# A two-block transformer kernel: input sums of the feed-forwards in another order, squares added on VectorE, x stored from ScalarE's queue and loaded ahead, the first pair's weight sums made sooner

## The chip, the cores and the metric

The kernel runs on one core of one Trainium2 chip. The metric is the device time of one execution in microseconds (us). The engines are TensorE (PE for matmuls, PEld for weight loads), VectorE (DVE), ScalarE (ACT), GpSimd (POOL) and SyncE (SP, which only issues DMAs). TensorE's granted clock has two levels here, 2.4 and 1.2 GHz; the profile gives it as a fraction of the higher one.

## The reference, cut to what matters

Two transformer blocks run on a sequence of 512 tokens with 1024 channels. The change touches the places where a residual sum ends and the next normalised feed-forward (or attention) begins:

```python
x = x + jnp.einsum('bsd,de->bse', merged, w_out[l])       # block 1, residual
h2 = rmsnorm(x, norm_mlp_g[l])
up = jnp.square(jax.nn.relu(jnp.einsum('bsd,df->bsf', h2, w_up[l])))
x = x + jnp.einsum('bsf,fd->bsd', up, w_down[l])
...
x = x + merged @ w_mix_out[l]                              # block 2
x = x + cross_attention(rms_norm(x, xattn_norm_g[l]), ...) # its last step is "@ w_o"
x = x + swiglu(rms_norm(x, ffn_norm_g[l]), w_ffn_gate[l], w_ffn_up[l], w_ffn_down[l])
```

`rmsnorm` divides by the root of the mean square over the channels and multiplies by a gain per channel.

## The kernel before, in words

Activations lie transposed: a tile has 128 channels on the partitions and 512 tokens along the row, so x is 8 tiles (m = 0 to 7). Every fp32 operand is split into a high and a low part (`split_to`, lines 269 to 276: the high part by a cast on ACT, the low part by a subtraction on DVE), and a product is three matmuls (`mm3`). A projection to one tile (`proj_T`) takes a weight slab of 128 x 1024: it is loaded into a `raw` buffer from SP's queue, cast to `wh` on ACT (L270) and subtracted to `wl` on DVE (L271), and 24 matmuls of 512 columns follow. There are 3 `raw`, 4 `wh` and 4 `wl` buffers; the DMAs of weights stay in program order on SP.

**Two transitions** are the subject. In the first, `residual_stage` multiplies by `w_out` (tiles m = 0 and 1 together in `proj_T_lead`, then m = 2 to 7), reloads x from DRAM tile by tile on POOL's queue (L681), adds it to the product in PSUM (L683, DVE), stores the new x to a DRAM buffer on POOL's queue (`put`, L319) and calls `norm_sums`. In the second, `residual_keep` does the same for `w_xo`, with x still on chip, so without the load (the addition is L1517). A third place, `residual_stage` with `w_mix`, loads x too but calls `norm_tile` and stores nothing.

`norm_sums` prepares the input of a feed-forward whose matrix products are made by a fast scheme with seven half-size products in place of eight (indices 1 to 7). An even tile gives `ae` = x times gain (ACT); an odd tile gives `ao`, and from the two come the sums `f1` and `f2` (four DVE operations on half tiles, L346 to L349) and the splits of `s1` (half of `ae`), `f1`, `f2` and `ao`. `square` takes x squared on ACT (L472) and adds it to a running sum on POOL (L474); `rstd_tok` makes the last addition (L484, POOL), sums over the channels by 8 small matmuls against ones, and makes the root in some ten small DVE operations and the diagonal tiles `dgh`, `dgl`; `rstd_row` turns these into a row by two matmuls.

`weight_sums` loads two weight slabs and makes the sums and splits for the same scheme (L367 to L378: four casts on ACT, eight operations on DVE, with one `wh`, two `wl`, two `sum` and four `big` buffers). `halves` calls it and then makes the seven products into the PSUM tiles `u`, `v` and `p2`. For the first two jobs of a feed-forward (`halves_lead`) the parts that need no more than tiles 0 to 6 of x come first: all of product 1, and three quarters of products 5 and 2. These are 30 matmuls of 256 columns for each job; the rest waits for the last odd tile.

Instructions are written in program order, and a scheduler fixes each engine's order beforehand, by program order and its own estimate of when inputs are ready. On the chip an engine runs its list in that order, so an instruction that waits holds up all behind it on its engine; the same holds for DMAs in an engine's queue. Buffers of one kind are handed out as earlier users are done.

Of the kernel before, what the change touches and what calls it, by code (L numbers as in the profile page):

```python
# [15 lines left out]
S = 512  # L16
# [78 lines left out]
class Net:  # L95
    def __init__(self, tc, I, out, opts=None):
        self.tc, self.nc, self.I, self.out = tc, tc.nc, I, out
        self.o = dict(

            raw=3, wh=4, wl=4, sum=2, big=8, slots=56,  # L100

            attn=54, attn2=77, tail=30, early=8, adelay=23.0, lru=387, fox=40, fd=15.0, swa=44, cross=45,

            lL=6.63, lu=3.2, lo=8.0, lg=1.25, f0=1.6, f1=2.8, f2=1.4, s0=2.4, s1=6.9, s2=3.4, x1=5.75, x2=2.5,
        )
        self.o.update(opts or {})
        self.n = 0
        self.clock = Clock()
        self.sq = None


    def name(self, s):
# [203 lines left out]
    def put(self, m, x):  # L316
        if m == 0:
            self.xs = self.dp.tile([8, P, S], F32, tag="xs", bufs=1, name=self.name("xs"))
        self.nc.gpsimd.dma_start(out=self.xs[m], in_=x)  # L319

    def get(self, m):
        x = self.T("x")
# [3 lines left out]
    def norm_sums(self, x, g, kt, sq, st):  # L326


        nc = self.nc
        H = S // 2  # L330
        if kt % 2 == 0:
            a = self.T("ae")
            nc.scalar.activation(a, x, AF.Copy, scale=self.col(g, kt))
            self.square(x, sq)
            st["even"] = a
            return
        e, o = st.pop("even"), self.T("ao")
        nc.scalar.activation(o, x, AF.Copy, scale=self.col(g, kt))
        self.square(x, sq)
        kp = kt // 2  # L340
        if kp % 2 == 0:
            st["one"] = (self.R("s1h"), self.R("s1l"))
        c = (kp % 2) * H
        s1 = tuple(t[:, c : c + H] for t in st["one"])
        f1, f2 = self.T("f1"), self.T("f2")
        nc.vector.tensor_sub(f1[:, :H], e[:, H:], o[:, H:])  # L346
        nc.vector.tensor_sub(f1[:, H:], f1[:, :H], e[:, :H])
        nc.vector.tensor_sub(f2[:, :H], e[:, :H], e[:, H:])
        nc.vector.tensor_add(f2[:, H:], o[:, :H], f1[:, H:])  # L349
        self.split_to(s1[0], s1[1], e[:, :H])  # L350
        p1, p2, po = self.split(f1, s="f1"), self.split(f2, s="f2"), self.split(o, s="ao")
        cut = lambda p, i: tuple(t[:, i * H : i * H + H] for t in p)
        st.setdefault("S", []).append(
            {1: s1, 2: cut(po, 0), 4: cut(po, 1), 5: cut(p1, 0), 6: cut(p1, 1), 7: cut(p2, 0), 3: cut(p2, 1)}
        )
# [36 lines left out]
    def halves(self, wname, j, st, out, lead=False):  # L392

        nc = self.nc
        H = S // 2
        w = self.weight_sums(wname, j)
        u, v, p2 = self.PS("u"), self.PS("v"), self.PS("p2")
        if lead:
            late = range(KT // 2 - 1, KT // 2)
            early = range(KT // 2 - 1)  # L400
        a, b = self.T("ca"), self.T("cb")
        self.product(u, st, w, 1, True)
        nc.scalar.copy(a[:, :H], u[:, :H])
# [12 lines left out]
        self.product(u, st, w, 6, False)  # L416
        nc.scalar.copy(b[:, :H], u[:, :H])
        yield
        self.product(u, st, w, 7, False)
        nc.scalar.copy(b[:, H:], u[:, :H])  # L420
        nc.vector.tensor_sub(b[:, H:], v[:, :H], b[:, H:])
        yield
        self.product(u, st, w, 4, False)
        nc.scalar.copy(a[:, H:], u[:, :H])
        self.product(v, st, w, 3, False)
        nc.vector.tensor_sub(b[:, :H], v[:, :H], b[:, :H])
        if lead:
            yield
        out(a, b)

    def halves_lead(self, jobs):

        a, b = jobs
        for _ in range(3):
            next(a)
            next(b)
        r = self.rstd_tok(self.sq)
        for g in (a, b, a):
            next(g)
        self.r, self.row = self.rstd_row(r)  # L440
        self.sq = None
        self.rounds((a, b))
# [21 lines left out]
        for f in fillers:  # L464
            f()

    def square(self, x, sq, n=S, at=0):

        nc = self.nc
        q = self.T("sq")  # L470
        sl = slice(at, at + n)
        nc.scalar.activation(q[:, sl], x[:, sl], AF.Square)  # L472
        if len(sq) == 2:
            nc.gpsimd.tensor_add(sq[0][:, sl], sq[0][:, sl], sq[1][:, sl])  # L474
            sq.pop()
        sq.append(q)

    def rstd_tok(self, sq, n=S, at=0, quick=False):

        nc = self.nc  # L480
        nt = n // P
        if len(sq) == 2 and not quick:
            sl = slice(at, at + n)
            nc.gpsimd.tensor_add(sq[0][:, sl], sq[0][:, sl], sq[1][:, sl])  # L484
            sq.pop()
# [88 lines left out]
    def block1(self):  # L574
# [74 lines left out]
        for m in range(8):  # L649
# [6 lines left out]
        self.residual_stage("w_out", mg, "norm_mlp_g", self.I["xT"], True)  # L656

    def until(self, gen, cond):

# [10 lines left out]
        for g in gens:  # L670
            yield from g

    def residual_stage(self, wname, act, g, reload, halves=False):

        nc = self.nc
        sq = []
        new, nact, st = [], [], {}
        pss = self.proj_T_lead([(wname, 0), (wname, 1)], act)
        for m in range(8):
            x = self.T("x")  # L680
            nc.gpsimd.dma_start(out=x, in_=reload[m])  # L681
            ps = pss[m] if m < 2 else run(self.proj_T(wname, m, act))
            nc.vector.tensor_add(x, ps, x)  # L683
            new.append(x)
            if halves:
                self.put(m, x)
                self.norm_sums(x, g, m, sq, st)
            else:
                nact.append(self.norm_tile(x, g, m, sq))
        self.x, self.act, self.sq = [None] * 8 if halves else new, st if halves else nact, sq  # L690

    def consts1(self):
        nc = self.nc
# [816 lines left out]
    def residual_keep(self, wname, act, g):  # L1510
# [263 lines left out]
```

## Time and profile before

| | |
|---|---|
| median of 3 runs | 1924.06 us (1923.16 to 1924.74) |
| profiled execution | 1925.78 us, span of its trace 1924.0 us |
| TensorE matmul busy | 1868.6 us (97%) |
| VectorE busy | 1371.2 us (71%) |
| ScalarE busy | 868.4 us (45%) |
| GpSimd busy | 271.1 us (14%) |
| mean granted TensorE clock | 0.985 |

Busy time counts an instruction from its start to its end. Matmuls overlap one another, so the distance between the starts of two matmuls is shorter than the duration of one, and busy PE time is not work at full speed. The number in brackets at the end of a line of a timeline is the time that the engine stood idle before it, and behind the arrow is what ended the wait.

### The profile page before, as it was taken

How to read it: one execution, taken by the hardware profiler on the slowest of the kernel's cores; microseconds unless marked ns; L12 is line 12 of the kernel's file. 1: busy time of each engine (PE TensorE's matmuls, PEld its weight loads, DVE VectorE, ACT ScalarE, POOL GpSimd, SP SyncE). 2: the span in 40 equal slices, each digit the busy share in tenths (PEclk: the TensorE clock that was granted, in tenths of full speed). 3: DMA queues.
4: the chain of work that ended last, by engine and by line, in shares of the span. 5: the costliest groups of instructions: out<-in, count | busy, mean ns of one | idle time of the engine just before them, and what ended most of it. 6: DMA issues, size and time to landing. Idle time of an engine off the chain costs nothing.

```text
span 1924.0 us, 26869 instructions
## 1 busy us (share of the span) xinstructions
PE 1868.6 (97%) x10376; PEld 1604.5 (83%) x10376; DVE 1371.2 (71%) x2570; ACT 868.4 (45%) x1499; POOL 271.1 (14%) x280
## 2 busy tenths in 40 slices
PE   8999989999989999999999999999999989999996
PEld 6787867877869999998887788888888889999896
DVE  7477777786688788777667856446556798887874
ACT  5265654464354334334334444233434555444443
POOL 2322220200330000002012110132200220000002
PEclk9999999999989999999999999999999999999998
DMA  5223222221344333334321122232432333323221
GB/s 180 70 86 98 92 85 77 88 70 52 127 147 132 98 100 101 97 99 142 106 78 66 66 83 72 99 121 98 147 128 88 115 115 121 112 98 109 89 91 53
DMA packets 56944, 192.23 MB, mean 100 GB/s; under 512 B 7040, under 2 KB 10144, under 8 KB 56816
## 3 DMA queue, kind: packets, MB, share of 16 engines
q1 hardware_dynamic: 50016, 170.78, 27.3%
q0 software_dynamic: 6112, 19.21, 3.2%
q8 instruction: 81, 1.33, 0.3%
q10 hardware_dynamic: 688, 0.53, 0.1%
q14 instruction: 47, 0.39, 0.1%
HBM read 182.06 MB, written 8.43 MB: 99 GB/s over the span
## 4 chain that ended last, share of the span: by engine, by line
PE 79%; DVE 11%; ACT 3%; issue 3%; DMA 2%; POOL 2%; SPq 0%; DVEq 0%; POOLq 0%; ACTq 0%
PE ps L159 56%; PE u L159 10%; PE v L159 5%; PE p L159 2%; PE s L159 2%; PE o L159 2%; DVE wl L271 1%; PE pv L159 1%; DMA raw<-in_w_fg 1%; PE pt L163 1%; DMA x<-in_xT 1%; ACT wh L270 1%; DMA raw<-in_w_fd 1%; DVE wl L372 1%; ACT L L823 0%
## 5 line engine op out<-in xcount | busy, mean ns | idle before, releaser
L159 PE MATMUL ps<-xx,wh 128*128 128x512 f32 x1424 | 447.7, 396 | 2.7 <-ACT wh L270 2.7
L270 ACT CAST wh<-raw 128x1024 fp32r<-128x1024 f32 (+4 forms) x252 | 255.2, 1017 | 341.8 <-PE ps L159 214.4
L271 DVE TENSOR_TENSOR wl<-raw,wh 128x1024 fp32r<-128x1024 f32 (+4 forms) x252 | 314.2, 1248 | 85.1 <-ACT wh L270 83.3
L159 PEld LDWEIGHTS ps<-xx,wh 128*128 128x128 f32 x1424 | 263.1, 189 | 59.3 <-ACT wh L270 3.1
L159 PE MATMUL ps<-xx,wl 128*128 128x512 f32 x712 | 279.0, 392 | 1.1 <-DVE wl L271 1.1
L159 PE MATMUL ps<-wh,xx 128*128 128x512 f32 (+1 forms) x512 | 158.0, 381 | 5.6 <-ACT wh L270 5.6
L159 PEld LDWEIGHTS ps<-xx,wl 128*128 128x128 f32 x712 | 134.3, 189 | 31.2 <-DVE wl L271 2.3
L159 PEld LDWEIGHTS ps<-wh,xx 128*128 128x128 f32 x512 | 95.8, 192 | 23.9 <-ACT wh L270 5.6
L474 POOL TENSOR_TENSOR sq<-sq,sq 128x512 f32<-128x512 f32 (+1 forms) x46 | 62.2, 1353 | 317.8 <-ACT sq L472 317.4
L159 PE MATMUL ps<-uh,wh 128*128 128x512 f32 x256 | 100.2, 391 | 0.0
L159 PE MATMUL ps<-ul,wh 128*128 128x512 f32 x256 | 100.1, 391 | 0.0
L159 PE MATMUL ps<-uh,wl 128*128 128x512 f32 x256 | 99.5, 389 | 0.0
L159 PE MATMUL ps<-wl,xx 128*128 128x512 f32 (+1 forms) x256 | 96.9, 379 | 1.2 <-DVE wl L271 1.2
L159 PE MATMUL ps<-fah,wh 128*128 128x512 f32 (+1 forms) x200 | 73.3, 368 | 0.0
L159 PE MATMUL ps<-fal,wh 128*128 128x512 f32 (+1 forms) x200 | 73.3, 366 | 0.0
L159 PE MATMUL ps<-fah,wl 128*128 128x512 f32 (+1 forms) x200 | 72.8, 364 | 0.0
L1043 DVE TENSOR_TENSOR x<-ps,x 128x512 f32<-128x512 f32 x64 | 44.0, 688 | 39.5 <-PE ps L159 39.5
L371 ACT CAST sah<-sa 128x1024 fp32r<-128x1024 f32 x38 | 39.9, 1051 | 59.1 <-DVE sa L369 57.8
L159 PE MATMUL v<-f2h,wl 128*128 128x256 f32 x304 | 60.9, 283 | 0.0
L1015 POOL TENSOR_TENSOR gt<-gt,gt 128x512 f32<-128x512 f32 x24 | 36.0, 1499 | 155.2 <-DVE gt L1011 155.2
L159 PEld LDWEIGHTS ps<-wl,xx 128*128 128x128 f32 x256 | 49.3, 193 | 9.8 <-DVE wl L271 2.0
L159 PEld LDWEIGHTS ps<-uh,wl 128*128 128x128 f32 x256 | 48.1, 188 | 10.2
(453 smaller groups left out, 4976.9 us busy)
## 6 DMA issues: line engine op xcount, KB each, us to landing
raw<-in_w_up SPq DMA_DIRECT2D x32, 512.0 KB, 3.5
raw<-in_w_down SPq DMA_DIRECT2D x32, 512.0 KB, 3.6
raw<-in_w_gate SPq DMA_DIRECT2D x24, 512.0 KB, 3.4
raw<-in_w_qkv SPq DMA_DIRECT2D x23, 512.0 KB, 3.6
raw<-in_w_fg SPq DMA_DIRECT2D x22, 512.0 KB, 3.4
raw<-in_w_fu SPq DMA_DIRECT2D x22, 512.0 KB, 3.4
raw<-in_w_fd SPq DMA_DIRECT2D x16, 512.0 KB, 3.4
raw<-in_w_conv SPq DMA_DIRECT2D x12, 512.0 KB, 3.5
```

Of the source, the lines that this page charges most:

```text
L159: self.nc.tensor.matmul(out, **k)
L163: self.nc.tensor.transpose(out, a, ident)
L270: nc.scalar.copy(hi, src)
L271: nc.vector.tensor_sub(lo, src, hi.bitcast(F32))
L371: nc.scalar.copy(ha, sa)
L372: nc.vector.tensor_sub(la, ra, h.bitcast(F32))
L474: nc.gpsimd.tensor_add(sq[0][:, sl], sq[0][:, sl], sq[1][:, sl])
L1015: nc.gpsimd.tensor_add(merged[m], merged[m], t)
L1043: nc.vector.tensor_add(self.x[m], ps, self.x[m])
```

## The change

It does five things. (1) `norm_sums` is in another order: for an even tile the split of `s1` is made at once; for an odd tile `ao` is split first, then `f1` is made and split, then `f2`, and the square comes last. (2) In `norm_sums` the running sum of squares is added on DVE in place of POOL, and `rstd_tok` (with `both=True`) leaves out the last addition: it runs its small matmuls over both remaining tiles. (3) `put` stores x from ACT's queue in place of POOL's, and in `norm_sums`, behind the scaling by the gain. (4) `residual_stage` issues the loads of x up to two tiles further ahead. (5) The first pair's weight sums (`w_up` or `w_fg`, j = 0) are made in program order ahead of the slab of tile m = 5, and `halves` takes them from `self.ready`.

```diff
     def put(self, m, x):
...
-        self.nc.gpsimd.dma_start(out=self.xs[m], in_=x)
+        self.nc.scalar.dma_start(out=self.xs[m], in_=x)
...
         if kt % 2 == 0:
-            a = self.T("ae")
-            nc.scalar.activation(a, x, AF.Copy, scale=self.col(g, kt))
-            self.square(x, sq)
-            st["even"] = a
+            e = st["even"] = self.T("ae")
+            nc.scalar.activation(e, x, AF.Copy, scale=self.col(g, kt))
+            self.put(kt, x)
+            if kp % 2 == 0:
+                st["one"] = (self.R("s1h"), self.R("s1l"))
+            c = (kp % 2) * H
+            st["s1"] = tuple(t[:, c : c + H] for t in st["one"])
+            self.split_to(st["s1"][0], st["s1"][1], e[:, :H])
+            self.square(x, sq, pool=False)
             return
-        e, o = st.pop("even"), self.T("ao")
+        e, o, s1 = st.pop("even"), self.T("ao"), st.pop("s1")
+        f1, f2 = self.T("f1"), self.T("f2")
         nc.scalar.activation(o, x, AF.Copy, scale=self.col(g, kt))
-        self.square(x, sq)
...
+        self.put(kt, x)
+        po = self.split(o, s="ao")
         nc.vector.tensor_sub(f1[:, :H], e[:, H:], o[:, H:])
         nc.vector.tensor_sub(f1[:, H:], f1[:, :H], e[:, :H])
+        p1 = self.split(f1, s="f1")
         nc.vector.tensor_sub(f2[:, :H], e[:, :H], e[:, H:])
         nc.vector.tensor_add(f2[:, H:], o[:, :H], f1[:, H:])
-        self.split_to(s1[0], s1[1], e[:, :H])
-        p1, p2, po = self.split(f1, s="f1"), self.split(f2, s="f2"), self.split(o, s="ao")
+        p2 = self.split(f2, s="f2")
+        self.square(x, sq, pool=False)
...
-        w = self.weight_sums(wname, j)
+        w = self.ready or self.weight_sums(wname, j)
+        self.ready = None
...
-        r = self.rstd_tok(self.sq)
+        r = self.rstd_tok(self.sq, both=True)
...
         if len(sq) == 2:
-            nc.gpsimd.tensor_add(sq[0][:, sl], sq[0][:, sl], sq[1][:, sl])
+            eng = nc.gpsimd if pool else nc.vector
+            eng.tensor_add(sq[0][:, sl], sq[0][:, sl], sq[1][:, sl])
...
-        if len(sq) == 2 and not quick:
+        if len(sq) == 2 and not quick and not both:
...
+        xs = []
+
+        def load():
+            if len(xs) < 8:
+                xs.append(self.T("x"))
+                nc.gpsimd.dma_start(out=xs[-1], in_=reload[len(xs) - 1])
+
+        for _ in range(2):
+            load()
         pss = self.proj_T_lead([(wname, 0), (wname, 1)], act)
         for m in range(8):
-            x = self.T("x")
-            nc.gpsimd.dma_start(out=x, in_=reload[m])
+            load()
+            x = xs[m]
+            if ahead is not None and m == 5:
+                self.ready = self.weight_sums(ahead, 0)
             ps = pss[m] if m < 2 else run(self.proj_T(wname, m, act))
             nc.vector.tensor_add(x, ps, x)
             new.append(x)
-            if halves:
-                self.put(m, x)
+            if ahead is not None:
                 self.norm_sums(x, g, m, sq, st)
...
         for m in range(8):
+            if m == 5:
+                self.ready = self.weight_sums("w_fg", 0)
             ps = pss[m] if m < 2 else run(self.proj_T(wname, m, act))
             nc.vector.tensor_add(self.x[m], ps, self.x[m])
-            self.put(m, self.x[m])
             self.norm_sums(self.x[m], g, m, sq, st)
```

## Rows read from the trace of the kernel before

**Rows 1.** The page, busy time of an engine, share, instructions.

```profile
PE 1868.6 (97%) x10376; PEld 1604.5 (83%) x10376; DVE 1371.2 (71%) x2570; ACT 868.4 (45%) x1499; POOL 271.1 (14%) x280
```

**Rows 2.** Stretches: length, busy time (instructions) by engine, clock, DMA share, GB/s.

```profile
521.10:554.20 33.10, 33.10 (x147) 27.40 (x146) 29.51 (x40) 20.28 (x29) 9.71 (x13) 1.00 0.49 159
554.20:587.60 33.40, 23.84 (x140) 22.37 (x139) 24.12 (x50) 16.43 (x30) 10.78 (x15) 0.74 0.48 158
521.10:587.60 66.50, 56.94 (x286) 49.77 (x285) 53.63 (x89) 36.72 (x57) 20.50 (x27) 0.87 0.48 158
1544.40:1574.20 29.80, 25.12 (x177) 24.10 (x175) 27.17 (x54) 16.76 (x27) 8.15 (x6) 0.89 0.35 122
1511.20:1574.20 63.00, 58.32 (x324) 51.57 (x322) 59.23 (x97) 39.27 (x61) 20.30 (x17) 0.95 0.38 133
597.00:1210.00 613.00, 611.46 (x3541) 528.32 (x3540) 445.85 (x866) 251.66 (x468) 49.58 (x56) 1.00 0.30 95
1210.00:1511.00 301.00, 301.00 (x1490) 255.65 (x1488) 164.43 (x239) 114.36 (x179) 47.42 (x46) 1.00 0.34 111
```

**Rows 3.** PE's waits from 515 to 620, the longest two: us in total, times, longest.

```profile
PE ps L159 <- POOL sq L484: 3.7, 1, 3.7
PE u L159 <- ACT s1h L270: 3.4, 2, 3.1
```

**Rows 4.** PE's waits from 1511 to 1620, the longest two.

```profile
PE ps L159 <- DVE dgh L506: 1.4, 1, 1.4
PE u L159 <- ACT s1h L270: 1.2, 1, 1.2
```

**Rows 5.** PE's timeline: matmuls of 256 columns at both clocks, the statistics.

```profile
563.96 0.41 PE L159 MATMUL v<-f1l,sah 128*128 128x256 f32 x1
564.17 0.41 PE L159 MATMUL v<-f1h,sal 128*128 128x256 f32 x1
...
1562.24 0.28 PE L159 MATMUL u<-f1l,sah 128*128 128x256 f32 x1
1562.36 0.28 PE L159 MATMUL u<-f1h,sal 128*128 128x256 f32 x1
...
1563.20 0.95 PE L159 MATMUL ps<-ones,sq 128*128 128x2 f32 x8
```

**Rows 6.** DVE's timeline, additions of x in the two transitions.

```profile
557.93 0.69 DVE L683 TENSOR_TENSOR x<-ps,x 128x512 f32<-128x512 f32 x1 [2.75 <-DMA x<-in_xT]
...
570.85 0.69 DVE L683 TENSOR_TENSOR x<-ps,x 128x512 f32<-128x512 f32 x1 [1.02 <-DMA x<-in_xT]
...
1550.02 0.68 DVE L1517 TENSOR_TENSOR x<-ps,x 128x512 f32<-128x512 f32 x1
```

**Rows 7.** POOL's timeline in the first transition.

```profile
543.10 1.51 POOL L474 TENSOR_TENSOR sq<-sq,sq 128x512 f32<-128x512 f32 x1 [0.58 <-ACT sq L472]
544.55 0.55 POOL L681 DMA_DIRECT2D x<-in_xT  x1
553.22 0.54 POOL L319 DMA_DIRECT2D xs<-x  x1 [8.12 <-DVE x L683]
553.75 0.54 POOL L681 DMA_DIRECT2D x<-in_xT  x1
```

**Rows 8.** Users of tile ae (ns, min/median/max), and DVE's timeline beside POOL's additions.

```profile
L347 DVE TENSOR_TENSOR f<-f,ae x8: 408/1502/1523, 529.1 to 1554.1; 128x256 f32<-128x256 f32 x8
...
543.39 1.50 DVE L347 TENSOR_TENSOR f<-f,ae 128x256 f32<-128x256 f32 x1
...
1535.31 2.25 DVE L377 TENSOR_TENSOR sbl<-sb,sbh 128x1024 fp32r<-128x1024 f32 x1
```

**Rows 9.** Issues of the output's stores on ACT's queue (ns, min/median/max).

```profile
L1600 ACTq DMA_DIRECT2D out_T<-out x2: 378/383/388, 1916.7 to 1917.5; - x2
```

**Rows 10.** DVE's timeline, the low parts of the last two slabs of w_out.

```profile
531.23 1.21 DVE L271 TENSOR_TENSOR wl<-raw,wh 128x1024 fp32r<-128x1024 f32 x1
...
534.17 1.21 DVE L271 TENSOR_TENSOR wl<-raw,wh 128x1024 fp32r<-128x1024 f32 x1
```

More of the change, by code (lines that the diff above doesn't have):

```diff
@@ L330, in norm_sums @@
         H = S // 2
+        kp = kt // 2
         if kt % 2 == 0:
-            a = self.T("ae")
-            nc.scalar.activation(a, x, AF.Copy, scale=self.col(g, kt))
-            self.square(x, sq)
-            st["even"] = a
+            e = st["even"] = self.T("ae")
[7 more added lines that the diff above has]
+            self.square(x, sq, pool=False)
             return
-        e, o = st.pop("even"), self.T("ao")
+        e, o, s1 = st.pop("even"), self.T("ao"), st.pop("s1")
+        f1, f2 = self.T("f1"), self.T("f2")
         nc.scalar.activation(o, x, AF.Copy, scale=self.col(g, kt))
-        self.square(x, sq)
[L340 to L345, printed above, removed]
+        self.put(kt, x)
+        po = self.split(o, s="ao")
         nc.vector.tensor_sub(f1[:, :H], e[:, H:], o[:, H:])
         nc.vector.tensor_sub(f1[:, H:], f1[:, :H], e[:, :H])
+        p1 = self.split(f1, s="f1")
         nc.vector.tensor_sub(f2[:, :H], e[:, :H], e[:, H:])
         nc.vector.tensor_add(f2[:, H:], o[:, :H], f1[:, H:])
-        self.split_to(s1[0], s1[1], e[:, :H])
-        p1, p2, po = self.split(f1, s="f1"), self.split(f2, s="f2"), self.split(o, s="ao")
+        p2 = self.split(f2, s="f2")
+        self.square(x, sq, pool=False)
         cut = lambda p, i: tuple(t[:, i * H : i * H + H] for t in p)
@@ L395, in halves @@
         H = S // 2
-        w = self.weight_sums(wname, j)
+        w = self.ready or self.weight_sums(wname, j)
+        self.ready = None
         u, v, p2 = self.PS("u"), self.PS("v"), self.PS("p2")
@@ L465, in fill, with square @@
             f()
-    def square(self, x, sq, n=S, at=0):
+    def square(self, x, sq, n=S, at=0, pool=True):
         nc = self.nc
@@ L473, in square, with rstd_tok @@
         if len(sq) == 2:
-            nc.gpsimd.tensor_add(sq[0][:, sl], sq[0][:, sl], sq[1][:, sl])
+            eng = nc.gpsimd if pool else nc.vector
+            eng.tensor_add(sq[0][:, sl], sq[0][:, sl], sq[1][:, sl])
             sq.pop()
         sq.append(q)
-    def rstd_tok(self, sq, n=S, at=0, quick=False):
+    def rstd_tok(self, sq, n=S, at=0, quick=False, both=False):
         nc = self.nc
         nt = n // P
-        if len(sq) == 2 and not quick:
+        if len(sq) == 2 and not quick and not both:
             sl = slice(at, at + n)
@@ L655, in block1 @@
             mg.append(self.gate_mul(gt[m], ps, merged, m, False, True))
-        self.residual_stage("w_out", mg, "norm_mlp_g", self.I["xT"], True)
+        self.residual_stage("w_out", mg, "norm_mlp_g", self.I["xT"], "w_up")
     def until(self, gen, cond):
@@ L671, in chain, with residual_stage @@
             yield from g
-    def residual_stage(self, wname, act, g, reload, halves=False):
+    def residual_stage(self, wname, act, g, reload, ahead=None):
         nc = self.nc
@@ L689, in residual_stage @@
                 nact.append(self.norm_tile(x, g, m, sq))
-        self.x, self.act, self.sq = [None] * 8 if halves else new, st if halves else nact, sq
+        self.x, self.act, self.sq = new if ahead is None else [None] * 8, nact if ahead is None else st, sq
     def consts1(self):
```

## The prediction

> **What bounds the kernel now.** I read the page first: TensorE is busy 97% of the span and VectorE 71% [rows 1], so only work that TensorE waits for can pay. Then the busy time by stretch, to find where TensorE is not full: from 597 to 1210 it is idle for 1.5 us in 613, from 1210 to 1511 for none. The two transitions are another matter: 9.6 idle us in the 33.4 from 554.2, and 4.7 in the 29.8 from 1544.4, with granted clocks of 0.74 and 0.89 [rows 2]. The third place of the change (w_mix) lies within 1210 to 1511, so nothing done there shows.
>
> Busy time hides a part of the loss, so I counted the matmuls. After its last projection TensorE has for the first two jobs, up to the row of the root, 30 early matmuls each, 6 late ones each, 12 each for products 6 and 7 and 12 of product 4 for one job: 2 x (30 + 6 + 24) + 12 = 132. At full clock two starts lie 0.12 us apart, at half clock 0.21 [rows 5]. So 132 x 0.12 = 15.8 us, with 0.95 us for the statistics 16.8 us; the stretch took 33.4. **The first transition loses 16.6 us.** In the second stretch 177 instructions less 8 of the statistics give 169 x 0.12 + 0.95 = 21.2 us of 29.8: **it loses 8.6 us.** Together 25.2 us is the most to be had here.
>
> The Trainium skill ("Trainium Kernel Development and Optimization", Performance Expectations) says that matmul busy time is a bad measure of how close a kernel is to its limit, because matmuls overlap. By busy time the ceiling would be 9.6 + 4.7 = 14.3 us; this trace's starts agree with the rule.
>
> Then who ends the waits. In the first transition they are ScalarE's s1h and GpSimd's last sum of squares [rows 3]. Both hang on x: VectorE adds the last x at 570.85, after a wait for its load, though TensorE had its product at 554.2 [rows 6]. The cause is in GpSimd's list: the load issued at 544.55 stood behind a sum of squares, the next one at 553.75 behind a store that waited 8.12 us for the x before [rows 7]. So each x waits for the one before, and the chain ends 16 us late. In the second transition x is on chip, and still TensorE waits longest for dgh, of VectorE, and for s1h [rows 4]; the last addition of x starts at 1550.02, 5.6 us after its product [rows 6], with no wait: VectorE is behind with its work (59.2 busy us of 63.0 [rows 2]). A second cause sits in both: half-tile operations that take 0.41 us at best have a median of 1.50, and one of 1.21 takes 2.25, while GpSimd adds squares: the one at 543.39 lies on the addition from 543.10 [rows 7, 8]. I count 6 such in the first transition (6.5 us too long in sum) and 7 in the second (7.0 us).
>
> **The change part by part.**
>
> *Loads ahead, stores moved.* Eight loads per stage (0.54 us each on GpSimd) now stand behind neither store nor squares, so the additions of x follow TensorE, one each 5.4 us (24 matmuls of 33.1/147 us). The last x of the first transition moves from 570.85 to about 554.5. Eight stores per stage move to ScalarE at 0.38 each [rows 9] (0.54 if they cost what they did on GpSimd): 3.0 to 4.3 us per stage on an engine busy 36.7 of 66.5 us [rows 2]. They wait for nothing new (the scaling ahead needs the same x); behind each stands the cast of ao. Uncovered, the last one of a stage is 0.4 us of the path; I take 0 because VectorE is later than ScalarE.
>
> *Squares on VectorE.* Six additions per stage at 0.69 us, from the addition of the same shape [rows 6]: +4.1 us. They wait for ScalarE's Square with the slab and weight work behind them; that is within the idle time below. In return GpSimd reads nothing in these stretches, so 6.5 and 7.0 us go. If only half of the lengthening were GpSimd's doing, the net would be +0.9 and +0.6 in place of -2.4 and -2.9; the overlap in time speaks for all of it.
>
> *Statistics over two tiles.* Eight more small matmuls, +0.95 us per transition on TensorE [rows 5]; the GpSimd addition that TensorE waited 3.7 us for [rows 3] goes.
>
> *Order of the sums.* Nothing is added; the splits that the late products need start up to one operation earlier. Worth 0 to 1 us, taken as 0.
>
> *Weight sums sooner.* The same 4 casts, 8 operations and 2 loads. The first job is ready before TensorE ends its projections; the loads pass three slab loads on SP's queue. The price is buffers: two of four wl are held, so a slab of tiles 5 to 7 can be made only when the projection two before it ends, 5.4 us ahead of need in place of 10.9. See the slow rival. Taken as 0.
>
> **The sum.** With x on time, who is late next? VectorE. *First transition:* 53.6 - 6.5 + 4.1 = 51.2 us of its work from 521.1, so 572.3 if it never waits. It will wait for ScalarE here and there; the nearest row is the second transition, with the same work and no loads: 63.0 - 59.2 = 3.8 us. So 576.1. TensorE's own bound is 554.2 + 16.8 + 0.95 = 572.0. The later rules: 587.6 - 576.1 = 11.5 us gained; bounds 8.0 (if it loses as much as the second does now, 16.6 - 8.6) and 15.6 (TensorE's bound). *Second:* 59.2 - 7.0 + 4.1 = 56.3 from 1511.2, so 1567.5, and with 3.8 of waiting 1571.3: 2.9 gained. About 1.2 us of that waiting was for TensorE's late product 2, which is now earlier, so I take 3.5; bounds 0 (the net of the squares is nothing and the order no better) and 7.6 (8.6 less 0.95). Sum 15 us. Against the profiled execution, 1925.8 us (span 1924.0 and 1.8 around it), that is 1910.8; the median of the runs is 1.7 lower, so **1909 us**. Some of the matmul records are missing from the trace, which makes my floor of TensorE low by well under 1 us.
>
> **The rivals.**
>
> *Nothing of TensorE's loss is left (15%).* VectorE's waits vanish because the new order feeds it better: both at TensorE's bound, 15.6 + 7.6 = 23 us, 1901. For it: ScalarE has room. Against: 51.2 us of 50.9 (521.1 to 572.0) is over 100% of VectorE.
>
> *The first becomes what the second is now, the second gains nothing (22%).* The fixed lists still put the second job's weight sums ahead of the last x on VectorE, as they do before 1550.02. 8 + 0 us, 1916.
>
> *The loads do not come earlier (3%).* The scheduler keeps them late on GpSimd's list, or they land late. Then only VectorE's net is left, and the chain of x stays: 0 to 3 us, 1923. Against: with stores and squares gone nothing else stands in that list.
>
> A page speaks for this last one: the Trainium skill ("SBUF — State Buffer", two separate sides) warns that DMAs issued from GpSimd can starve while VectorE holds the port pair that they share. The issues here last 0.54 to 0.55 us in a VectorE stretch that is nearly full [rows 2, 7], which does not bear it out.
>
> *Slabs come late (5%, the slow side).* Place: the slabs of tiles 5 to 7 in both stages. Today the last two are done 5.3 and 2.8 us after their buffer is free (527.1 to 532.4, 532.6 to 535.4 [rows 10]); with 5.4 us until TensorE needs them, a fuller VectorE that answers 2 us later makes TensorE wait, and a wait here is followed by a stretch at half clock (some 27 matmuls x 0.09 = 2.5 us in the first transition). Six slabs x (2 + 2.5) = 27 us against a gain of 15: 1936. It decides from 2.5 us of lateness per slab, or 0.7 if the clock drops each time. Against: casts and loads are done well before, and the slab's operation stands ahead of the later sums in program order.
>
> **How the numbers follow.** The forecast has 55%, with its own range of 1904 to 1913. To leave out no more than 2 in 10 the range takes in the rival at 1916 and the one at 1901: 1901 to 1918. About 0.2%, 3.9 us, is what a measurement can tell from no change. Faster: 55 + 15 + 22, less a little of the last for smaller gains, and none of the others: 0.90. Same: the late loads and that little: 0.05. Slower: the slabs, 0.05.
>
> **What would show it.** Right: the last x of the first transition added near 555 with no wait for a load; no VectorE operation lengthened in the two transitions; GpSimd's list there with loads alone; TensorE's clock above 0.9 from 554 on; the root's row some 11 us earlier in the first and 3 to 4 in the second transition; from then on to the next transition unchanged lengths. Wrong: waits of TensorE for wl in the tiles 5 to 7; VectorE idle over 4 us per transition; weight sums ahead of the last x on VectorE; a gain in the stretch of w_mix.

## The result and the profile after

The changed kernel takes 1912.39 us (median of 4 runs, 1911.61 to 1914.38) against 1924.4 us beside it (1923.16 to 1928.2). The ratio is 0.9936 with a 95% interval of 0.9919 to 0.9953: faster by 12 us, inside the range, 3.4 us above the forecast of 1909. Its profiled execution took 1914.38 us, its span 1912.6 us.

Two lengths carry the argument from here on. **First** is the time from the start of the last projection matmul ahead of the first transition (`ps<-mgh,wl`) to the first product of the down projection (`ps<-uh,wh`); **second** is the time from the last projection matmul ahead of the second transition (`ps<-xoh,wl`) to ScalarE's copy of the root's row. Before, they are 554.00 to 596.88 = 42.9 us and 1544.15 to 1575.38 = 31.2 us; after, 552.76 to 590.01 = 37.3 us and 1537.47 to 1563.75 = 26.3 us. So the first gave 5.6 us (11.5 forecast) and the second 5.0 (3.5 forecast). Between the two lie 947.3 us before and 947.5 after, behind them 348.6 and 348.9. Of the 11.4 us by which the spans differ, 1.2 more lie ahead of the first transition, and the stretches between and behind the two give 0.4 back.

The stretches of the kernel after, as in [rows 2] (length, busy time and instructions by engine, clock, DMA share, GB/s):

```profile
519.40:552.80 33.40, 33.40 (x149) 27.32 (x148) 30.77 (x51) 23.80 (x34) 0.00 (x0) 1.00 0.47 164
552.80:583.00 30.20, 25.25 (x166) 24.14 (x165) 21.25 (x49) 13.86 (x24) 2.68 (x5) 0.83 0.40 122
1537.50:1563.70 26.20, 23.88 (x166) 23.02 (x165) 21.58 (x51) 12.30 (x22) 1.09 (x2) 0.87 0.29 98
590.00:1203.00 613.00, 611.45 (x3540) 528.04 (x3539) 446.07 (x867) 251.51 (x468) 49.60 (x56) 1.00 0.30 94
1203.00:1504.00 301.00, 301.00 (x1491) 255.60 (x1490) 170.39 (x246) 116.07 (x181) 48.59 (x46) 1.00 0.32 111
```

The last two rows are as full as before: nothing was to be had there. In the transitions GpSimd is nearly empty, yet TensorE still idles for 5.0 and 2.3 us, its granted clock is 0.83 and 0.87, and VectorE is busy for only 21.3 of 30.2 us. GpSimd's timeline shows the eight loads of x in a row, far ahead, where [rows 7] had a store that waited 8.12 us; the rows behind are reloads of x for the next stage, which come early now:

```profile
511.47 4.27 POOL L689 DMA_DIRECT2D x<-in_xT  x8
555.13 0.54 POOL L324 DMA_DIRECT2D x<-xs  x1 [39.39 <-ACT sq L477]
556.27 0.54 POOL L324 DMA_DIRECT2D x<-xs  x1 [0.60 <-ACT s1h L271]
557.50 0.54 POOL L324 DMA_DIRECT2D x<-xs  x1 [0.70 <-DVE sq L480]
```

VectorE's timeline: the last x of the first transition is added at 555.93 without a wait (570.85 in [rows 6]). But then VectorE itself waits, for f1h and for the statistics:

```profile
555.93 0.68 DVE L700 TENSOR_TENSOR x<-ps,x 128x512 f32<-128x512 f32 x1
...
561.41 0.41 DVE L350 TENSOR_TENSOR f<-f,ae 128x256 f32<-128x256 f32 x1
...
565.60 0.69 DVE L272 TENSOR_TENSOR f1l<-f,f1h 128x512 fp32r<-128x512 f32 x1 [1.79 <-ACT f1h L271]
...
571.38 0.16 DVE L500 TENSOR_SCALAR s<-ps 128x4 f32<-128x4 f32 x1 [3.04 <-PE ps L160]
...
1544.85 0.41 DVE L350 TENSOR_TENSOR f<-f,ae 128x256 f32<-128x256 f32 x1
```

TensorE's timeline says where its time goes now (at half clock two starts are 0.21 us apart, as in [rows 5]):

```profile
565.62 0.50 PE L160 MATMUL v<-f1h,sah 128*128 128x256 f32 x2 [2.60 <-ACT f1h L271]
...
568.20 3.15 PE L160 MATMUL ps<-ones,sq 128*128 128x2 f32 x14 [0.80 <-ACT sq L477]
...
572.63 0.41 PE L160 MATMUL u<-f1h,sah 128*128 128x256 f32 x1
572.84 0.41 PE L160 MATMUL u<-f1l,sah 128*128 128x256 f32 x1
...
1547.89 0.39 PE L160 MATMUL v<-f1l,sah 128*128 128x256 f32 x1 [1.08 <-DVE f1l L272]
...
1549.75 3.15 PE L160 MATMUL ps<-ones,sq 128*128 128x2 f32 x14 [1.11 <-ACT sq L477]
```

And ScalarE's timeline says why f1h and the last square are late:

```profile
557.40 0.62 ACT L271 CAST aoh<-ao 128x512 fp32r<-128x512 f32 x1
564.00 1.04 ACT L271 CAST wh<-raw 128x1024 fp32r<-128x1024 f32 x1 [5.98 <-DMA raw<-in_w_down]
564.95 0.61 ACT L271 CAST f1h<-f 128x512 fp32r<-128x512 f32 x1
...
567.52 0.63 ACT L477 ACTIVATE sq<-x 128x512 f32<-128x512 f32 x1
...
1544.69 1.05 ACT L371 CAST wh<-raw 128x1024 fp32r<-128x1024 f32 x1 [2.94 <-DMA raw<-in_w_fu]
1545.65 0.61 ACT L271 CAST f1h<-f 128x512 fp32r<-128x512 f32 x1
...
1548.54 0.62 ACT L271 CAST f2h<-f 128x512 fp32r<-128x512 f32 x1 [1.55 <-DVE f L353]
1549.07 0.62 ACT L477 ACTIVATE sq<-x 128x512 f32<-128x512 f32 x1
```

In the first transition the cast of a slab that is still on its way (w_down) stands in the list ahead of f1h, so f1h, f2h and the last square wait for a DMA that they have nothing to do with. VectorE had both halves of f1 ready at 561.8 (L349 and L350); f1h starts at 564.95. In the second the cast of a slab (w_fu) stands there too, but it holds f1h back by only 0.4 us, since VectorE ends the second half of f1 at 1545.26. There the last square is late because it stands behind f2h, and f2h waits 1.55 us for VectorE's f2.

### The profile page after: what moved, and what is told of

Read it like the earlier page. It is cut to its first block, busy times and chain, and to the rows that moved or that the text cites. A ratio compares the mean times of both kernels' runs of the same rounds, so it can differ in the third digit from the quotient of the medians.

```text
span 1912.6 us, 26867 instructions
## 1 busy us (share of the span) xinstructions
PE 1866.2 (98%) x10392; PEld 1603.7 (84%) x10392; DVE 1367.2 (71%) x2582; ACT 867.8 (45%) x1499; POOL 238.6 (12%) x250
## 4 chain that ended last, share of the span: by engine, by line
PE 79%; DVE 11%; ACT 4%; DMA 3%; issue 2%; POOL 1%; DVEq 0%; SPq 0%; ACTq 0%; POOLq 0%
PE ps L160 56%; PE u L160 10%; PE v L160 4%; PE p L160 2%; PE s L160 2%; PE o L160 2%; DVE wl L272 2%; PE pv L160 1%; PE pt L164 1%; DMA raw<-in_w_fg 1%; ACT wh L271 1%; ACT L L839 0%; DMA raw<-in_w_fd 0%; PE ps L164 0%; PE ut L164 0%
## 5 line engine op out<-in xcount | busy, mean ns | idle before, releaser
L160 PEld LDWEIGHTS ps<-xx,wl 128*128 128x128 f32 x712 | 134.3, 189 | 31.2 <-DVE wl L272 2.3
L480 POOL TENSOR_TENSOR sq<-sq,sq 128x512 f32<-128x512 f32 (+1 forms) x34 | 41.3, 1217 | 307.3 <-ACT sq L477 307.0
L160 PEld LDWEIGHTS ps<-uh,wh 128*128 128x128 f32 x256 | 48.2, 188 | 9.3 <-ACT uh L271 0.4
```

Source lines behind the costliest of these rows:

```text
L160: self.nc.tensor.matmul(out, **k)
L480: eng.tensor_add(sq[0][:, sl], sq[0][:, sl], sq[1][:, sl])
```

## The experiments

Twelve kernels were run, in three sets, each beside runs of the kernel before. Since these drift by 0.1% from set to set, the ratio is what is compared. One thousandth is 1.9 us.

| kernel | time (us) | ratio, interval | first | second |
|---|---|---|---|---|
| before | | 1 | 42.9 | 31.2 |
| after | 1912.39 | 0.9936 (0.9919 to 0.9953) | 37.3 | 26.3 |
| u2: after, squares on GpSimd | 1910.63 | 0.9923 (0.9908 to 0.9937) | 32.7 | 28.8 |
| u3: after, stores on GpSimd | 1912.30 | 0.9927 (0.9913 to 0.9942) | 35.1 | 22.0 |
| u4: after, loads not ahead | 1925.06 | 0.9995 (0.9985 to 1.0004) | 47.9 | 24.7 |
| u5: after, sums not sooner | 1912.60 | 0.9939 (0.9922 to 0.9955) | 34.6 | 28.0 |
| b1: before, loads ahead | 1916.07 | 0.9950 (0.9936 to 0.9964) | 32.9 | 31.2 |
| g1: after, reloads behind the row | 1915.50 | 0.9939 (0.9926 to 0.9952) | 31.3 | 24.9 |
| s1: after, last sum on VectorE | 1915.28 | 0.9937 (0.9925 to 0.9949) | 34.5 | 30.6 |
| u1: after, old order | 1898.71 | 0.9855 (0.9841 to 0.9868) | 28.7 | 22.1 |
| a1: after, squares at their old place | 1901.69 | 0.9884 (0.9867 to 0.9900) | 30.2 | 21.8 |
| b2: u1, square of the odd tile last | 1903.00 | 0.9881 (0.9868 to 0.9893) | 27.7 | 25.0 |
| c1: b1, squares on VectorE | 1903.16 | 0.9882 (0.9869 to 0.9895) | 31.0 | 22.4 |
| d1: u1, squares on GpSimd | 1909.84 | 0.9915 (0.9903 to 0.9927) | 30.6 | 28.2 |

The lengths are of one profiled execution each, and that one can lie up to 5 us off the median (u3: 1907.85 against 1912.30; g1: 1910.26 against 1915.50). The stretch behind the second (345 to 350 us) varies by some us from kernel to kernel, so a length shows where, and the ratio how much.

### First set: one part of the change undone at a time

**u2**, squares and last addition back on GpSimd:

```diff
-            self.square(x, sq, pool=False)      # both places in norm_sums
+            self.square(x, sq)
-        r = self.rstd_tok(self.sq, both=True)
+        r = self.rstd_tok(self.sq)
```

> The changed kernel with its part 2 undone: the running sums of squares are added on GpSimd again, and the last addition is made there before 8 small matmuls in place of 16. Theory (GpSimd's additions lengthen VectorE's half-tile operations, and VectorE sets the end of both transitions): operations of 0.41 us read 1.5 us again, some 6 per transition, and the kernel is 3 to 6 us slower than the changed one (1915 to 1918). Rival (VectorE stands idle some 8 us in the first transition of the changed kernel, so its operations are not what ends it; the 16 small matmuls are): not slower than the changed kernel, or 1 to 3 us faster (1909 to 1912).

Not slower. My step on the squares fell, for this order of the sums: in the changed kernel VectorE isn't the bound, so what they save on it buys nothing. In u2 some half-tile operations are long again (s1l up to 1.52 us), and TensorE waits 2.87 us for s1l in the first transition; but its waits there for f1h and the square are gone.

**u3**, stores back on GpSimd's queue:

```diff
-        self.nc.scalar.dma_start(out=self.xs[m], in_=x)
+        self.nc.gpsimd.dma_start(out=self.xs[m], in_=x)
```

> The changed kernel with its part 3 undone in the queue alone: x is stored from GpSimd's queue, the loads still ahead. Theory (a load only has to stand ahead of the store of the tile before it): the additions of x in the first transition still follow the products, last one at 555 to 557, total within 1.5 us of the changed kernel (1911 to 1914). Rival (any store in the list holds up the loads): the last x comes 3 us or more later, total 1915 or more.

No difference that can be told, as the prediction had it for the stores. But ScalarE's list is another one: here f1h and f2h stand ahead of the slab's cast, and only the last square behind it.

```profile
560.33 0.62 ACT L271 CAST f1h<-f 128x512 fp32r<-128x512 f32 x1 [2.23 <-DVE f L350]
562.81 0.62 ACT L271 CAST f2h<-f 128x512 fp32r<-128x512 f32 x1 [1.86 <-DVE f L353]
564.57 1.05 ACT L271 CAST wh<-raw 128x1024 fp32r<-128x1024 f32 x1 [1.14 <-DMA raw<-in_w_down]
...
566.73 0.62 ACT L477 ACTIVATE sq<-x 128x512 f32<-128x512 f32 x1
```

So u3 is as slow as the changed kernel without a wait of TensorE for f1h. Its waits are 1.53 us for s1h, 0.81 for s1l and 0.76 for the last square in the first transition, and 1.69 for the last square in the second.

**u4**, the two loads ahead taken out:

```diff
-        for _ in range(2):
-            load()
```

> The changed kernel with its part 4 undone: each load of x is issued in program order at its own tile again, while stores and squares are off GpSimd's queue. Theory (it was stores and squares in the list that made loads late; with an empty list they go out by themselves): additions of x as in the changed kernel, total within 1.5 us of it (1911 to 1914). Rival (loading ahead in program order carries the gain): the last x of the first transition 3 us or more later, total 1915 or more.

The whole gain goes. GpSimd's timeline shows that program order alone holds the loads back, with nothing else in the list:

```profile
510.78 3.22 POOL L689 DMA_DIRECT2D x<-in_xT  x6
537.20 0.54 POOL L689 DMA_DIRECT2D x<-in_xT  x1 [23.20 <-DVE sq L480]
547.57 0.54 POOL L689 DMA_DIRECT2D x<-in_xT  x1 [9.84 <-PE ps L160]
```

Loads 7 and 8 wait for releases by VectorE and TensorE. That fits the code: the x tiles come from one pool with all others of their size, so a tile asked for two steps later gets a later slot. In VectorE's list the later additions are late as well (the fifth starts at 556.02, the last at 570.93), and the first transition is 47.9 us long. No addition waits for its load, though; the additions stand late in VectorE's list itself. The fifth stands behind weight sums, with VectorE at work without a marked wait from 542.8 to 559.8. That the scheduler put them there because it reckoned with late loads is likely, but not shown.

**u5**, weight sums at their old place (both calls ahead of m = 5 taken out):

```diff
-                self.ready = self.weight_sums(ahead, 0)
...
-                self.ready = self.weight_sums("w_fg", 0)
```

> The changed kernel with its part 5 undone: the first pair's weight sums stand behind all input sums in program order again. Theory (the sums of the first pair were early enough before; buffers make the difference nil): within 1.5 us of the changed kernel (1911 to 1914). Rival (with x on time the first pair's sums compete with the last input sums on VectorE, so TensorE waits for them): 3 to 8 us slower (1915 to 1920), with waits of TensorE for sah or wl just behind the projections.

No difference: worth nothing in time, as forecast.

### Second set: what holds the first transition

After the first set the loads carried the gain, and nothing explained the 6 us that the first transition lacked. My theory was that the early reloads hold up the w_down slab.

**g1**, reloads behind the row, by a one-column copy on GpSimd that reads the row first:

```diff
-    def get(self, m):
+    def get(self, m, after):
         x = self.T("x")
+        self.nc.gpsimd.tensor_copy(x[:, :1], after[:, :1])
```

> The changed kernel, with a one-column copy on GpSimd ahead of each of the eight reloads of x for the feed-forward's result, that reads the root's row; so no reload is issued before the row is there (three are issued at 555 to 557.5 us in the changed kernel). Theory B1 (the early reloads share the DMA engines with the first slab of w_down, which landed 6.1 us after its issue; ScalarE's cast of that slab stands in its list ahead of f1h, for which TensorE waited 2.6 us): the slab lands in 3.5 to 4 us, ScalarE's wait for it falls from 6.0 to 3.5 us, TensorE's wait for f1h goes, its clock does not fall, and the time is 1908 to 1910 us. Rival (the slab lands late for another reason, or the cast alone holds f1h back): landing and wait as they are, 1911 to 1914 us. A third outcome: the reloads come too late for the down projection, waits of the additions behind it, over 1914 us.

The mechanism was there: slab loads landed in 3.5 us (median of two; 4.8 after), ScalarE waited 2.23 us in place of 5.98, and the first transition fell from 37.3 to 31.3 us. TensorE's wait for f1h went, as expected; but it waited 1.10 us for f1l and 1.12 for the square, and its clock still fell (0.80 from 564 to 568). And the time stayed. The third outcome came with it: from the down projection's first product to the second transition it takes 951.4 us in place of 947.5. The reloads are issued only from 579.1 us on, at the start of the down projection (TensorE's longest wait in that stretch, which the changed kernel doesn't have):

```profile
PE u L160 <- ACT cb L423: 2.2, 1, 2.2
```

So 3.9 us were given back there. The profiled execution is still the fastest of the five (1910.26 us), and over all of them the interval shows no gain; what the slower ones lost is not shown. The collision is one cause of the slab's lateness, but in this form not a lever.

**s1**, one more addition on VectorE, 8 small matmuls:

```diff
+        q = self.sq
+        self.nc.vector.tensor_add(q[0], q[0], q[1])
+        q.pop()
-        r = self.rstd_tok(self.sq, both=True)
+        r = self.rstd_tok(q)
```

> The changed kernel with one more addition of squares on VectorE per transition, so that the statistics take 8 small matmuls on TensorE in place of 16 (3.15 us at half clock in both transitions, 0.95 us for 8 at full clock before). Theory (the 16 matmuls are a term of the transitions): minus 1 to minus 2 us per transition, 1908 to 1911 us. Rival (TensorE waits for the last square in any case, and one more addition of 0.69 us on VectorE stands in that chain, so the small matmuls only start later): 1911 to 1914 us, TensorE's wait for sq longer by 0.7 us.

The rival: no gain. In this run the statistics stand later in TensorE's list (573.00, 8 in 0.95 us); f1h is waited for as before (2.0 us). Fewer small matmuls bought nothing.

**b1**, part 4 of the change alone, in the kernel before (the diff of `load` as in the change; nothing else):

> The kernel before with one part of the change alone: in the first transition the loads of x are issued two tiles ahead of the tile that adds them. Squares and stores stay on GpSimd's list, the sums keep their old order, the first weight sums their old place. Theory A (the loads carry the whole gain; it is shared out over both transitions only because VectorE's order after the first is better): 1912 to 1916 us, last x addition of the first transition before 558 us of the span, root's row near 583, first product of the down projection near 590 (596.9 before). Theory B (squares and stores on GpSimd's list still lengthen VectorE's half-tile operations and hold the loads back, so that the parts are needed together): 1919 to 1924 us, last addition later than 562, half-tile operations on VectorE of 1.5 us still there. In either case the second transition has no load of x, so its length (row at 64.1 us after the first addition of x there) should stay within 1 us of before; then theory A is capped at a gain of about 7 us, 1917 us.

Theory A in the transitions: 10.0 us of the first, nothing of the second. In time the ratio says 9.6 us, more than the cap of 7. Two details were missed: the last x is added at 559.27, not before 558, and some half-tile operations still take 1.5 us, which was theory B's sign. The loads alone give the first transition more than the whole change did (5.6), so some other part takes back.

**u1**, the old order of the sums in `norm_sums`, all else as changed:

```diff
         self.put(kt, x)
-        po = self.split(o, s="ao")
+        self.square(x, sq, pool=False)
         nc.vector.tensor_sub(f1[:, :H], e[:, H:], o[:, H:])
         nc.vector.tensor_sub(f1[:, H:], f1[:, :H], e[:, :H])
-        p1 = self.split(f1, s="f1")
         nc.vector.tensor_sub(f2[:, :H], e[:, :H], e[:, H:])
         nc.vector.tensor_add(f2[:, H:], o[:, :H], f1[:, H:])
-        p2 = self.split(f2, s="f2")
-        self.square(x, sq, pool=False)
+        self.split_to(s1[0], s1[1], e[:, :H])
+        p1, p2, po = self.split(f1, s="f1"), self.split(f2, s="f2"), self.split(o, s="ao")
```

> The changed kernel with the old order of the input sums in each pair: squares ahead of the splits, s1 and the three pairs of splits at the end; stores behind the scaling, squares on VectorE and the rest as in the changed kernel. Theory (the order is worth nothing, as the prediction has it): within 2 us of the changed kernel, 1910 to 1914 us; f1 and f2 later by one to two operations (0.6 to 1.3 us), the statistics sooner by as much. Rival (the order is what made the second transition 4.9 us shorter, since s1h and dgh were what TensorE waited for there): 1915 to 1919 us, row of the second transition 62 to 64 us after the first addition of x there (59.2 in the changed kernel).

Neither theory: far faster than both, 0.0081 under the changed kernel, 15.6 us (11 to 20 by the two intervals). The new order is not worth nothing, it costs 15.6 us. The two profiled spans differ by 15.9 us: nearly 13 lie in the two lengths, 3.7 behind the second. ScalarE's timeline in this kernel has the square at once and the slab's cast last:

```profile
556.88 0.61 ACT L476 ACTIVATE sq<-x 128x512 f32<-128x512 f32 x1
560.13 0.62 ACT L271 CAST f1h<-f 128x512 fp32r<-128x512 f32 x1 [2.63 <-DVE f L350]
561.06 0.62 ACT L271 CAST f2h<-f 128x512 fp32r<-128x512 f32 x1 [0.32 <-DVE f L352]
561.59 0.61 ACT L271 CAST aoh<-ao 128x512 fp32r<-128x512 f32 x1
562.81 1.05 ACT L271 CAST wh<-raw 128x1024 fp32r<-128x1024 f32 x1 [0.61 <-DMA raw<-in_w_down]
```

Its statistics need no wait, and the stretches of its two transitions are nearly full, at full clock (the first row is the stretch ahead of the first):

```profile
519.50:552.90 33.40, 33.40 (x147) 27.13 (x147) 30.94 (x52) 24.61 (x37) 0.00 (x0) 1.00 0.46 156
552.90:574.60 21.70, 20.47 (x166) 19.91 (x165) 20.73 (x49) 12.83 (x22) 2.67 (x5) 1.00 0.54 177
1529.50:1551.60 22.10, 22.10 (x182) 21.87 (x181) 20.86 (x50) 12.74 (x22) 1.09 (x2) 1.00 0.37 132
```

From the last projection matmul to the row the first transition takes 30.3 us after and 21.8 in u1, 8.5 less. TensorE's waits make 4.95 - 1.23 = 3.7 of it; 33 matmuls at half clock, each 0.09 us longer, 3.0; the statistics at half clock (3.15 for 14, 1.84 for 16 in u1) 1.3. That is 8.0 of 8.5.

### Third set: which half of the order, and with what

**a1**, only the squares back at their old place (behind the scaling), the splits in the new order:

```diff
         self.put(kt, x)
+        self.square(x, sq, pool=False)
         po = self.split(o, s="ao")
...
         p2 = self.split(f2, s="f2")
-        self.square(x, sq, pool=False)
```

> The changed kernel with the squares of each tile put right behind its scaling and store again, as in the kernel with the whole order undone (1898.7 us); the new order of the splits stays (s1 with the even tile, then ao, f1, f2). Theory S (the place of the square carries the loss: TensorE's 16 small matmuls wait for the last Square, which the new order puts at the end of ScalarE's list, and the clock falls there): 1898 to 1903 us, statistics without a wait, row of the second transition 55 to 56 us after the first addition of x there. Theory P (the order of the splits carries it: ao ahead of f1 lets the cast of the w_down slab pass f1h in ScalarE's list): 1908 to 1913 us, TensorE still waits 2 to 3 us for f1h in the first transition.

**b2**, the converse, u1 with the odd tile's square behind the splits:

> The kernel with the whole order undone (1898.7 us), with only the odd tile's square moved behind the three splits, as the change has it. Theory S (the place of the square carries the loss): back to 1906 to 1913 us, 16 small matmuls behind a wait for sq, 2 to 3 us at half clock. Theory P (the order of the splits carries it): stays at 1898 to 1902 us. Both in part: 1903 to 1906 us.

From after to a1 the ratio falls by 0.0052 (10 us), from after to b2 by 0.0055 (10.6 us), and each lacks about 5 us to u1. So neither theory alone. Measured from u1 the new splits cost 5.6 us (a1) and the odd tile's late square 5.0 (b2; the even tile's stays at its old place there), each 1.5 to 10 by the intervals; both moves together cost 15.6. Whether that is more than the sum of the two can't be told from these times. ScalarE's timelines show what each move does. In a1 f1h is ahead of the slab's cast though ao is split first:

```profile
559.93 0.62 ACT L271 CAST f1h<-f 128x512 fp32r<-128x512 f32 x1 [2.82 <-DVE f L351]
561.99 1.04 ACT L271 CAST wh<-raw 128x1024 fp32r<-128x1024 f32 x1 [1.43 <-DMA raw<-in_w_down]
562.94 0.61 ACT L271 CAST f2h<-f 128x512 fp32r<-128x512 f32 x1
```

In b2 the square is the last of the tile, yet ahead of the cast:

```profile
560.53 0.63 ACT L476 ACTIVATE sq<-x 128x512 f32<-128x512 f32 x1
...
562.77 1.05 ACT L271 CAST wh<-raw 128x1024 fp32r<-128x1024 f32 x1 [1.08 <-DMA raw<-in_w_down]
```

In the changed kernel, with both moves, the slab's cast stands ahead of f1h and the square behind them all. But u3 has both moves too, and there f1h comes first. So the place of that cast doesn't follow from the two moves alone; why the scheduler puts it where it does is not shown. The clock in a1 and b2 stays at 1.00 from 552 to 580, as in u1.

**c1**, before with loads ahead and squares on VectorE (parts 4 and 2 alone; the edit of u2 turned round, on b1):

> The kernel before with two parts alone: loads of x ahead, and squares added on VectorE with the statistics over two tiles; stores stay on GpSimd's list, the sums keep their old order, the first weight sums their old place. If stores and early weight sums are worth nothing, as they were with the new order (1912.3 and 1912.6 against 1912.4 us), this is as fast as the kernel with only the order undone: 1897 to 1902 us. Rival (with the transitions tight, the stores on GpSimd or the later weight sums count again): 1903 to 1910 us, TensorE's wait in a transition over 3 us.

The rival by its number, but not by its reason: no wait is over 1.3 us. Its ratio is 0.0027 above u1's (5 us, some 2 to 9 by the intervals, and from another set), so with the old order stores and early sums may be worth something together; the lengths (31.0 and 22.4 against 28.7 and 22.1) put it in the first transition. Which of the two stays open. Against b1 the squares bring 0.0068 (13 us), 8.8 us of them in the second transition:

```profile
PE ps L159 <- DVE dgh L506: 1.4, 1, 1.4
PE u L159 <- ACT s1h L270: 1.2, 1, 1.2
```

These are TensorE's longest waits there in b1, the very ones of [rows 4]; c1 has neither.

**d1**, u1 with the edit of u2:

> The kernel with the order undone (1898.7 us), squares and the last sum back on GpSimd, 8 small matmuls. It closes a table of two by two: new order with squares on VectorE 1912.4, new order with squares on GpSimd 1910.6, old order with squares on VectorE 1898.7. Theory V (in the old order the squares on VectorE pay what the prediction worked out, because half-tile operations are lengthened beside GpSimd's additions): 1907 to 1916 us, half-tile operations of 1.5 us on VectorE there again, TensorE waiting for s1h and f1. Rival (the squares cost nothing in either order): 1897 to 1902 us.

Theory V by the time: 0.0060 above u1, 11.5 us, with waits for aoh, aol and dgh in the second transition (0.8 + 1.2 + 1.4 us). Not all half-tile operations are at 1.5 us again (median 411 ns, the longest 1508, for L350). But six of VectorE's operations from the first addition to the row of the second transition are lengthened, four of them half-tile, by 5.9 us in sum, and VectorE is busy longer there, though it has the six additions of squares less. First d1, then u1:

```profile
1497.50:1558.60 61.10, 57.68 (x330) 51.08 (x329) 54.64 (x94) 37.40 (x60) 12.68 (x9) 0.97 0.43 138
```

```profile
1496.50:1551.60 55.10, 55.10 (x328) 49.18 (x327) 49.59 (x97) 35.56 (x58) 1.09 (x2) 1.00 0.41 144
```

The table of two by two:

| ratio | squares on GpSimd | squares on VectorE |
|---|---|---|
| old order | 0.9915 | 0.9855 |
| new order | 0.9923 | 0.9936 |

The squares on VectorE pay 11.5 us with the old order and nothing with the new one; the new order costs 15.6 us with the squares on VectorE and nothing that can be told with them on GpSimd. u1 beats both the kernel before and the changed one, by 28 and 15.6 us.

## Why the prediction was right, and where it was wrong

*The bound.* Right in the main. The middle stretch is 947.2 to 947.9 us in every kernel but g1; the one behind the second transition, 345.1 us in u1 against 348.6 before, gave a few us as well. The floors from matmul counts hold: 21.2 + 0.95 us for the second transition, and u1 does it in 22.1, all busy at full clock. The estimated losses, 16.6 and 8.6 us, were nearly all there to be had: u1 recovers 14.1 us of the first length, and its second stretch is 7.7 us shorter (29.8 to 22.1), which is 8.6 less 0.95.

*Loads ahead.* Right in place and size. The last x at 555.93 (554.5 forecast), 10.0 us by itself (b1). My ground against the rival of the late loads (nothing else stands in GpSimd's list) was wrong, though: u4's list has nothing else either, and two loads are issued late.

*Stores, early weight sums.* Taken as 0, and undone one by one in the changed kernel they make no difference that can be told (u3, u5); with the old order c1 leaves some microseconds open. The store's issue costs 0.33 us on ScalarE. The slow rival fell: no wait of TensorE for a slab of tiles 5 to 7. (Its two thresholds were not on one footing: 2.5 us per slab is where the gain of 15 is eaten up without the clock, 0.7 is where the kernel would be 3.9 us slower with it.)

*Squares on VectorE.* The arithmetic held: half-tile operations are at their best duration, where [rows 8] had a median of 1502 ns (users of tile ae; ns, least, median, most):

```profile
L350 DVE TENSOR_TENSOR f<-f,ae x8: 411/416/426, 529.5 to 1544.9; 128x256 f32<-128x256 f32 x8
```

VectorE's work in the first transition up to the row was forecast as 51.2 us; u1 has 30.94 + 20.73 = 51.7. What followed from it did not hold for this kernel: u2 is no slower.

*Statistics over two tiles.* 0.95 us more was right at full clock (16 in 1.84 us in u1); at half clock and behind a wait they are 3.15 us after 0.80. In s1 half as many bought nothing.

*VectorE as the next bound.* Wrong for the changed kernel, which shows the sign that I had named: over 4 us idle in the transition (1.79 and 3.04 are the longest). The bound is right for u1, where VectorE is busy 20.73 of 21.70 us up to the row.

*Order of the sums.* **This is the step that failed.** "Worth 0 to 1 us, taken as 0": measured, it costs 15.6 us (u1 against after). I read the new order only for when VectorE's inputs are ready. I did not follow ScalarE's list: the square moved from the front to behind three splits, ao's cast came first, and in the changed kernel a cast that waits for a DMA came ahead of f1h. Where I asked of the stores what is queued behind them, I did not ask it here. That the order costs 15.6 us is shown; that the wait for the slab does it all is not. That wait explains the 2.60 us for f1h in the first transition, while u3, where f1h does not stand behind the slab's cast, is as slow. What the changed kernel and u3 share is the late last square: it starts 11.6 and 10.7 us after the last x in the first transition, 1.4 us after it in u1.

*The sum.* 15 us forecast, 10.6 in the transitions. It came near by luck, through errors of opposite sign. The row of the first transition, forecast some 11 us earlier, comes 4.1 us earlier after the last projection matmul (34.4 us before, 30.3 after). Without the order the change gives 28 us (ratio 0.9855), about what my rival "nothing of TensorE's loss is left" had (1901 us; u1 took 1898.7), which I held at 15%; the order then took 15.6 back. That rival's end is real, but not its reason, which was that the new order feeds VectorE better: u1 reaches it with the old order. My reason against it (VectorE at over 100%) was too strict: in u1 VectorE keeps up.

*TensorE's clock.* "Above 0.9 from 554 on" was wrong: 0.83. It goes with the waits for f1h and the square; without them, in u1, it is 1.00.

## What to carry to other kernels

When a change moves an instruction in program order, find its new neighbours on its own engine's list, and ask which of them waits, for a DMA or for another engine: all behind that one inherits the wait. Undo the parts of a change one by one, but read them in pairs as well: here one part was worth 11.5 us or nothing, depending on another that looked free. And a load issued "ahead" in code is ahead only if its buffer is free: see in the trace when the issues really come, and where the instructions that use the loads stand.

## What the runs showed of the hardware

A short wait of TensorE can cost more than itself. After the wait of 2.60 us for f1h the granted clock fell to its lower level, 1.2 GHz, and matmuls were 0.21 us apart until 576.7, over the further wait of 0.80 us for the square; in the second transition waits of 1.08 and 1.11 us were followed by the same, until 1556.3. The granted clock is the number behind the five busy times:

```profile
552.80:562.70 9.90, 8.57 (x68) 8.12 (x67) 9.75 (x17) 4.45 (x8) 1.61 (x3) 1.00 0.68 209
571.20:576.70 5.50, 5.50 (x27) 5.50 (x28) 4.04 (x17) 2.26 (x3) 0.54 (x1) 0.50 0.21 60
1552.90:1556.30 3.40, 3.40 (x16) 3.40 (x17) 2.35 (x13) 0.81 (x1) 0.41 (x1) 0.50 0.34 108
```

The length of a wait doesn't decide it alone. A wait of 1.23 us in u1 left the clock at 1.00, and so did waits of 0.79 and 1.22 us close together in d1's first transition and one of 1.69 us in u3's second. So the order's 8.5 us in the first transition are 3.7 us of waiting and about 4.3 of lower clock.

Three reloads of x beside it made a slab's load slower: the w_down load issued at 557.89 was waited for until 564.00, 6.1 us, where the page has a median of 3.5. In g1, with no reload beside it, the same slab was there after 3.4 us (555.56 to 559.00).

In these traces VectorE's half-tile operations are lengthened beside GpSimd's arithmetic, not beside its DMA issues. The issues at 555.13 to 557.50 took 0.54 us each while VectorE was busy for 5.00 of 5.00 us (555 to 560), and the half-tile operation at 557.73, beside the last of them, took 0.41 us. The Trainium skill ("SBUF — State Buffer", two separate sides) warns that DMAs issued from GpSimd can starve while VectorE runs an operation in a two-port mode, such as a copy of fp32 within SBUF. VectorE's operations in this stretch were all TENSOR_TENSOR, with no such copy, so it does not test the warning; nor does the stretch before the change that the prediction held against it, which has no copy either.
